# Rows of the matmuls' moving operands 32 bytes further apart

## The chip, the cores and the metric

The kernel runs on one core of a Trainium2 chip. The core has a matrix engine (TensorE, PE in the profile, with its weight loads shown apart as PEld), a vector engine (DVE), a scalar engine (ACT), GpSimd (POOL) and a sync engine (SP) that issues the DMAs here. Each engine runs its own list of instructions, and semaphores hold it where it needs another's result. A matmul on PE takes a weight block of 128 x 128 values that a weight load puts in place, and streams a second operand past it, the moving operand: here 256 columns, mostly. Both lie in the on-chip memory SBUF, which has 128 partitions; "address" below is a byte within a partition, the same in all of them. Results go to the accumulator memory PSUM.

The metric is the time of one execution on the device in microseconds, shorter being better.

## The reference, cut to what matters

A backbone of two layers is run on two groups of tokens that share the parameters: 128 context tokens and 128 latent tokens, which here lie side by side as the 256 columns of every moving operand. Layer 0 mixes tokens with multi-head latent attention and grouped-query attention side by side, layer 1 with differential attention; both are followed by a gated feed-forward part with a short convolution. What the changed rows feed are the large projections:

```python
h = rmsnorm(x, g_norm_mix[l]) * (1 + sc1) + sh1      # 2048 features
m, new = mixer_ab(h, ...)   # proj = h @ w_in ... out = concat(out_a, out_b) @ w_out
x = x + gt1 * m
h = rmsnorm(x, g_norm_ffn[l]) * (1 + sc2) + sh2
u = h @ w_up                                          # 2048 -> 2 * 5632
u = conv3(u) + b_conv; gate, val = split(u)
x = x + gt2 * ((silu(gate) * val) @ w_down)           # 5632 -> 2048
```

All inputs and outputs are float32.

## The kernel before, in words

**Two halves of every operand.** TensorE takes a reduced float32 format (`F32R`), so the kernel splits each operand into a rounded part and the rest: `split` copies the source into the high part on ACT (L194) and subtracts it on DVE for the low part (L195). `gemm` then makes three matmuls for each block k of 128 input features: high weights by high activations (L240), high weights by low activations (L241), low weights by high activations (L242), all added up in one PSUM bank. The next block follows directly. Each matmul has its own weight load, so in time the load for the next matmul runs beside the streaming of this one.

**Where the operands lie.** Weights come by DMA into `raw` (8 KB of a partition), are split into the tiles `wh` and `wl` of eight blocks of 512 bytes each, four buffers of each. Activations lie in three tiles whose rows (one for each k) hold 256 high values, then 256 low ones, 2048 bytes in all:

- `hx`, 16 rows: the normalised and modulated input of the mixers and of both feed-forward parts (`modulate`, L439 on ACT and L441 on DVE or POOL), and, under the same tag, the attention output `o` of layer 0 (`head_ab`);
- `oall`, 16 rows: the attention output of layer 1;
- `g`, 22 tiles of one row: the gated activations of half a feed-forward part, which the down projection reads.

The tiles `ql` and `kv_in` of layer 0's second projections are built in the same way, and the change leaves them alone.

In the compiled program the first row of `hx` lies at byte 43616, the `g` tiles from byte 182752 on in steps of 2048, `oall` at 163392, the `wh` buffers at 118752 and every 4096 after it, `wl` at 135136 and every 4096 after it. A row of 2048 bytes, a low half 1024 bytes behind its high half, a weight block of 512 bytes and a weight buffer of 4096 are all multiples of 512. So the distance of a moving row's start from a weight block's start, taken modulo 512, is one number for a whole tile: 128 for `hx`, 0 for `g`, 96 for `oall`. "Place" below means this number.

**Order.** The program runs layer 0's mixer (stage "ab", to about 500 us), its feed-forward part ("ffn0", to about 1250), layer 1's mixer ("c", to about 1700) and its feed-forward part ("ffn1"). In a feed-forward part, `up` (matmuls on `hx`) and `down` (matmuls on `g`) alternate, each twice. The order of work on every engine is decided when the program is built, by tile dependencies and a planner that places the modulation work (`row_step`, `feature_step`) between the projections; it does not depend on addresses. The gemms' results are taken from PSUM by ACT or DVE, with three buffers.

```python
pe.matmul(ps[:, :n], wh, xh(k), start=(i == 0), stop=False)
pe.matmul(ps[:, :n], wh, xl(k), start=False, stop=False)
pe.matmul(ps[:, :n], wl, xh(k), start=False, stop=(i == last))
```

Of the kernel before, what the change touches and what calls it, by code (L numbers as in the profile page):

```python
# [10 lines left out]
F32 = mybir.dt.float32  # L11
# [8 lines left out]
KD = D // P  # L20
T = 128
NT = 2 * T
NL = 2
GRID_W = 64
EPS = 1e-6
# [49 lines left out]
def step_kernel(ctx: ExitStack, tc: tile.TileContext, A: dict):  # L75
# [22 lines left out]
    def T_(pl, shape, tag, dt=F32, bufs=None):  # L98
        kw = {} if bufs is None else {"bufs": bufs}
        return pl.tile(shape, dt, tag=tag, name=nm(tag), **kw)  # L100
# [92 lines left out]
    def split(out_hi, out_lo, src):  # L193
        act.copy(out_hi, src)  # L194
        dve.tensor_tensor(out=out_lo, in0=src, in1=out_hi.bitcast(F32), op=ALU.subtract)  # L195
# [229 lines left out]
    def modulate(hx, rb, l, which, chunks):  # L425

        for c in chunks:
            h = T_(tmp, [P, NT], "nt", bufs=4)
            dve.tensor_tensor(out=h, in0=x[:, c], in1=rb, op=ALU.mult)
            for g in range(2):  # L430
                s = slice(g * T, (g + 1) * T)
                a_ = scl[:, l, which, c, g:g + 1]
                b_ = mod[:, l, 3 * which, c, g:g + 1]
                if g == 0:
                    dve.tensor_scalar(out=h[:, s], in0=h[:, s], scalar1=a_, scalar2=b_,  # L435
                                      op0=ALU.mult, op1=ALU.add)
                else:
                    act.activation(h[:, s], h[:, s], AF.Identity, scale=a_, bias=b_)
            act.copy(hx[:, c, :NT], h)  # L439
            eng = pool if c % 2 else dve  # L440
            eng.tensor_tensor(out=hx[:, c, NT:], in0=h, in1=hx[:, c, :NT].bitcast(F32),  # L441
                              op=ALU.subtract)

    def modulated(st, l, which, units):
        ensure(l, 3 * which + 1)
        ensure(l, 3 * which)
        hx = T_(keep, [P, KD, 2 * NT], "hx", F32R)
        modulate(hx, norm_scale(st), l, which, range(KD))
        fill(units)
        return hx  # L450
# [48 lines left out]
    def head_ab(pl, pairs, rs, v, hx, c):  # L499

        s = T_(ppool["att"], [P, 512], "att", bufs=3)
        for g, ks in ((0, slice(0, T)), (1, slice(T, 3 * T))):
            for i, (q, k) in enumerate(pairs):
                pe.matmul(s[:, ks], q[:, g * T:(g + 1) * T], k[:, ks],  # L504
                          start=(i == 0), stop=(i == len(pairs) - 1))
        mx = T_(small, [P, 2], "mx")
        sums = T_(small, [P, 2], "sums")
        p = T_(pl, [P, 3 * T], "p", bufs=2)
        softmax_parts(s, mx, sums, rs, None, p)
        rec = T_(small, [P, 2], "rec")  # L510
        dve.reciprocal(out=rec, in_=sums)
        dve.tensor_scalar(out=p[:, :T], in0=p[:, :T], scalar1=rec[:, 0:1], scalar2=None, op0=ALU.mult)
        dve.tensor_scalar(out=p[:, T:], in0=p[:, T:], scalar1=rec[:, 1:2], scalar2=None, op0=ALU.mult)
        yield
        pT = transposed(pl, p)
        yield
        o = T_(ppool["att"], [P, 512], "att", bufs=3)
        pe.matmul(o[:, 0:T], v(0), pT[:, 0:T], start=True, stop=True)
        pe.matmul(o[:, T:NT], v(1), pT[:, T:2 * T], start=True, stop=False)
        pe.matmul(o[:, T:NT], v(2), pT[:, 2 * T:], start=False, stop=True)  # L520
        split(hx[:, c, :NT], hx[:, c, NT:], o[:, :NT])


    def mixer_ab(hx, rb0, st):
        l = 0
        with tc.tile_pool(name="ab", bufs=1) as ab:
            with tc.tile_pool(name="abp", bufs=1) as pj:
# [106 lines left out]
                for q in range(4):  # L634
                    ensure(0, 1, [q])
                    ensure(0, 0, [q])
                    ada["both"] = False
                    pinned[0] = q == 3
                    if q == 3:
                        caches()  # L640
                    modulate(hx, rb0, 0, 0, range(4 * q, 4 * q + 4))
                    for c in range(23):
                        ps = gemm(W.chunk(), lambda k: hx[:, 4 * q + k, :NT], lambda k: hx[:, 4 * q + k, NT:])
                        to = pr[:, c] if c < 15 else qb[:, c - 15]
                        if q == 0:
                            act.copy(to, ps)
                        else:
                            dve.tensor_tensor(out=to, in0=to, in1=ps, op=ALU.add)
                        if q == 3:
                            finish(c)  # L650
                        if q < 3:
                            pump(RATE["in"], until=2 * (q + 2))
                        else:
                            pump(RATE["in3"])

            with tc.tile_pool(name="abh", bufs=1) as hp:
                ada["pew"] = PEW["heads"]

                o = T_(keep, [P, KD, 2 * NT], "hx", F32R)
                load_cw(0)  # L660
                WQ = Weights(A["w_q_up"], 6, 2)
                WK = Weights(A["w_kv_up"], 4, 4)
# [67 lines left out]
        ensure(l, 2)  # L730
        ada["pew"] = PEW["out0"]
        W = Weights(A["w_out_ab"], KD, 1)
        oh, ol = (lambda k: o[:, k, :NT]), (lambda k: o[:, k, NT:])
        for c in range(KD):
            fine[0] = c >= KD - QUIET[1]
            residual(gemm(W.chunk(), oh, ol, first=8), l, 0, c, st)
# [3 lines left out]
    def mixer_c(cp, hx, st):  # L740
# [10 lines left out]
                                 op0=ALU.add, op1=ALU.subtract)  # L751

        W = Weights(A["w_in_c"], KD, 1)
        xh, xl = (lambda k: hx[:, k, :NT]), (lambda k: hx[:, k, NT:])
        outs = []
        o_all = T_(cp, [P, KD, 2 * NT], "oall", F32R)

        def project(h):
            q = T_(cp, [P, 2, NT], "dq", bufs=2)
# [27 lines left out]
        def attend(h, q, k, v):  # L787
# [47 lines left out]
                    pe.transpose(pt[:, i * NT + g * T:i * NT + (g + 1) * T],  # L835
                                 on[:, g, i * P:(i + 1) * P], ident)
            src = pt.rearrange("p (i t) -> p i t", i=2)
            split(o_all[:, 2 * h:2 * h + 2, :NT], o_all[:, 2 * h:2 * h + 2, NT:], src)

        for h in range(8):  # L840
            start(attend(h, *project(h)))
# [1 line left out]

        ensure(l, 2)
        W = Weights(A["w_out_c"], KD, 1)
        oh, ol = (lambda k: o_all[:, k, :NT]), (lambda k: o_all[:, k, NT:])
        for c in range(KD):
            fine[0] = c >= KD - QUIET[2]
            residual(gemm(W.chunk(), oh, ol), l, 0, c, st)
# [5 lines left out]


    def ffn(hx, l, st):
        xh, xl = (lambda k: hx[:, k, :NT]), (lambda k: hx[:, k, NT:])
        W = Weights(A["w_up"][l], KD, 1)
        WD = Weights(A["w_down"][l], KQ, TB)  # L860
        cw = ada["cw"]
        with tc.tile_pool(name=f"ffn{l}", bufs=1) as fp, banks(f"pffn{l}") as pf:
            feat["home"], feat["pool"] = fp, pf

            def conv(ps, m):
                y = T_(fp, [P, NT], "cv", bufs=3)
                act.activation(y, ps, AF.Identity, scale=cw[:, 1, m:m + 1], bias=cw[:, 3, m:m + 1])  # L867
                y3 = y.rearrange("p (g t) -> p g t", g=2)
                p3 = ps.rearrange("p (g t) -> p g t", g=2)
                dve.scalar_tensor_tensor(out=y3[:, :, 1:], in0=p3[:, :, :T - 1],  # L870
                                         scalar=cw[:, 0, m:m + 1], in1=y3[:, :, 1:],
                                         op0=ALU.mult, op1=ALU.add)
                dve.scalar_tensor_tensor(out=y3[:, :, :T - 1], in0=p3[:, :, 1:],  # L873
                                         scalar=cw[:, 2, m:m + 1], in1=y3[:, :, :T - 1],
                                         op0=ALU.mult, op1=ALU.add)
                return y

            def up(q):
                gs = []
                for i in range(q * KQ, (q + 1) * KQ):  # L880
                    rate = 0 if i < LATE else FRATE["up"]
                    fine[0] = False
                    gate = conv(gemm(W.chunk(), xh, xl), i)
                    pump(0, rate)
                    if i == 0:
                        load_row()
                    val = conv(gemm(W.chunk(), xh, xl), NFF + i)
                    pump(0, rate)
                    act.activation(gate, gate, AF.Silu)
                    dve.tensor_tensor(out=val, in0=gate, in1=val, op=ALU.mult)  # L890
                    g = T_(fp, [P, 2 * NT], "g", F32R, bufs=KQ)
                    split(g[:, :NT], g[:, NT:], val)
                    gs.append(g)
                return gs

            def down(gs, q):
                for c in range(KD):
                    quiet = q == NQ - 1 and c >= KD - QUIET[0]
                    fine[0] = quiet
                    ps = gemm(WD.chunk(), lambda k: gs[k][:, :NT], lambda k: gs[k][:, NT:])  # L900
                    residual(ps, l, 1, c, st if q == NQ - 1 else None)
                    pump(0, 0 if quiet else FRATE["down"])

            for q in range(NQ):
                gs = up(q)
                if q == 0:
                    ensure(l, 5)
                down(gs, q)
            while feat["i"] < FLIMIT[stage[0]]:
                feature_step()  # L910


    with banks("pab") as ppool["ada"]:
# [5 lines left out]
        st = stat_init()  # L919
        for c in range(KD):  # L920
            stat_add(st, x[:, c], KD)
        hx = T_(keep, [P, KD, 2 * NT], "hx", F32R)
        rb0 = norm_scale(st)
        st = stat_init()
        mixer_ab(hx, rb0, st)
# [150 lines left out]
```

## Time and profile before

| what | us |
|---|---|
| median of three runs | 2488.23 |
| lowest and highest | 2485.64, 2488.37 |
| the profiled execution, whole | 2491.76 |
| its span, first to last instruction | 2489.7 |
| PE busy in it | 2424.8 (97%) |
| DVE busy | 1767.7 (71%) |
| ACT busy | 1155.9 (46%) |
| POOL busy | 167.2 (7%) |

The profiled execution lies 3.5 us above the median of the runs. Matmuls are pipelined: one is shown as 0.28 us long while the next starts about 0.12 us after it, so the sum of the matmuls' lengths says nothing of the time they take; the distance between starts does. How many matmuls start in a window of known length gives that distance. A count of a window also holds those that were still running at its left edge, 0.28 / 0.12, or 2.4 on average.

### The profile page before, as it was taken

What the parts mean: (1) busy time and instruction counts of PE and PEld (TensorE: products, weight loads), DVE (VectorE), ACT (ScalarE), POOL (GpSimd) and SP (SyncE); (2) the same over time, 40 slices, a digit from 0 to 9 for tenths busy, and PEclk for the clock granted to TensorE, in tenths of its full rate; (3) what the DMA queues carried; (4) which work ended last, traced back from release to release, by engine and by line L of the source; (5) the groups of instructions that cost most, each with busy time, mean ns of one, the idle gap of its engine ahead of it and who ended that gap; (6) DMA issues with size and microseconds to landing.
All of it is one profiled execution on the core that took longest, in us unless ns stands there. A gap on an engine that the chain in (4) does not pass through costs nothing.

```text
span 2489.7 us, 47301 instructions
## 1 busy us (share of the span) xinstructions
PE 2424.8 (97%) x19664; PEld 2284.3 (92%) x19664; DVE 1767.7 (71%) x2699; ACT 1155.9 (46%) x1815; POOL 167.2 (7%) x211
## 2 busy tenths in 40 slices
PE   6999999999999999999999999999999999999997
PEld 4778768799999999999979999897999999999997
DVE  2457534578898999999869897766897655666644
ACT  4335544455453345544455454345555434555442
POOL 2002101100000000001110101021000000000011
PEclk9999999999999999999999999999999999999999
DMA  9886677876667767677776777757665555555553
GB/s 380 310 318 242 233 266 305 307 267 252 253 251 266 300 255 259 252 268 259 279 272 246 271 250 277 265 206 284 245 236 185 185 185 187 187 187 185 182 179 115
DMA packets 92549, 612.92 MB, mean 246 GB/s; under 512 B 9968, under 2 KB 17840, under 8 KB 20400
## 3 DMA queue, kind: packets, MB, share of 16 engines
q1 hardware_dynamic: 92336, 609.91, 66.9%
q8 instruction: 154, 2.52, 0.4%
q14 instruction: 59, 0.48, 0.1%
HBM read 605.12 MB, written 4.75 MB: 245 GB/s over the span
## 4 chain that ended last, share of the span: by engine, by line
PE 94%; DMA 2%; issue 1%; DVE 1%; ACT 1%; POOL 0%; POOLq 0%; SPq 0%; DVEq 0%; ACTq 0%
PE acc L240 29%; PE acc L241 29%; PE acc L242 29%; PE ada L333 4%; DMA araw<-w_ada 1%; PE att L504 1%; DMA ckc<-cache_ckv 1%; PE ada L281 1%; DMA raw<-w_in_ab 0%; PE att L794 0%; PE att L494 0%; DMA raw<-w_ada 0%; DVE x L945 0%; PE ada L268 0%; DVE nt L435 0%
## 5 line engine op out<-in xcount | busy, mean ns | idle before, releaser
L194 ACT CAST wh<-raw 128x1024 fp32r<-128x1024 f32 (+1 forms) x788 | 791.8, 1010 | 1116.3 <-PE acc L241 956.1
L195 DVE TENSOR_TENSOR wl<-raw,wh 128x1024 fp32r<-128x1024 f32 (+1 forms) x788 | 924.9, 1182 | 469.1 <-ACT wh L194 466.4
L240 PE MATMUL acc<-hx,wh 128*128 128x256 f32 x4208 | 1191.5, 285 | 10.2 <-ACT hx L439 9.5
L241 PE MATMUL acc<-hx,wh 128*128 128x256 f32 x4208 | 1190.3, 283 | 0.0
L242 PE MATMUL acc<-hx,wl 128*128 128x256 f32 x4208 | 1189.3, 283 | 0.0
L240 PEld LDWEIGHTS acc<-hx,wh 128*128 128x128 f32 x4208 | 793.7, 189 | 47.5 <-ACT hx L439 19.7
L241 PEld LDWEIGHTS acc<-hx,wh 128*128 128x128 f32 x4208 | 795.0, 189 | 21.0 <-issue 19.4
L242 PEld LDWEIGHTS acc<-hx,wl 128*128 128x128 f32 x4208 | 795.2, 189 | 12.2 <-issue 12.1
L241 PE MATMUL acc<-g,wh 128*128 128x256 f32 x1408 | 398.1, 283 | 0.0
L242 PE MATMUL acc<-g,wl 128*128 128x256 f32 x1408 | 397.9, 283 | 0.0
L240 PE MATMUL acc<-g,wh 128*128 128x256 f32 x1408 | 397.7, 283 | 0.0
L318 DVE CUSTOM_DVE_ANT_0 junk<-araw,condb 128x2048 f32<-128x2048 f32 x120 | 274.8, 2290 | 0.0
L241 PEld LDWEIGHTS acc<-g,wh 128*128 128x128 f32 x1408 | 270.3, 192 | 0.0
L242 PEld LDWEIGHTS acc<-g,wl 128*128 128x128 f32 x1408 | 270.2, 192 | 0.0
L240 PEld LDWEIGHTS acc<-g,wh 128*128 128x128 f32 x1408 | 270.1, 192 | 0.0
L160 POOL TENSOR_TENSOR sqacc<-sqacc,sq 128x256 f32<-128x256 f32 x76 | 88.0, 1158 | 1613.1 <-issue 1282.1
L333 PE MATMUL ada<-araw,condw 128*32 128x512 f32 x864 | 124.4, 651 | 20.4 <-DMA araw<-w_ada 19.6
L362 DVE SCALAR_TENSOR_TENSOR aacc<-araw,condw,aacc 128x512 f32<-128x512 f32 x150 | 107.8, 748 | 0.3
L455 DVE SCALAR_TENSOR_TENSOR x<-acc,mod,x 128x128 f32<-128x128 f32 x192 | 58.3, 345 | 63.2 <-PE acc L242 63.2
L867 ACT ACTIVATE cv<-acc,convw 128x256 f32<-128x256 f32 x176 | 98.6, 560 | 0.0
L873 DVE SCALAR_TENSOR_TENSOR cv<-acc,convw,cv 128x254 f32<-128x254 f32 x176 | 84.3, 479 | 3.7
L870 DVE SCALAR_TENSOR_TENSOR cv<-acc,convw,cv 128x254 f32<-128x254 f32 x176 | 83.7, 476 | 0.0
(195 smaller groups left out, 1625.9 us busy)
## 6 DMA issues: line engine op xcount, KB each, us to landing
araw<-w_ada SPq DMA_DIRECT2D x188, 1024.0 KB, 5.9
raw<-w_up SPq DMA_DIRECT2D x176, 1024.0 KB, 4.8
raw<-w_down SPq DMA_DIRECT2D x88, 1024.0 KB, 4.8
raw<-w_in_c SPq DMA_DIRECT2D x48, 1024.0 KB, 5.1
raw<-w_in_ab SPq DMA_DIRECT2D x20, 1024.0 KB, 7.2
raw<-w_out_ab SPq DMA_DIRECT2D x16, 1024.0 KB, 5.2
raw<-w_out_c SPq DMA_DIRECT2D x16, 1024.0 KB, 4.8
raw<-w_q_up SPq DMA_DIRECT2D x6, 768.0 KB, 4.7
```

The costliest lines, as they stand in the source:

```text
L160: pool.tensor_tensor(out=st["acc"], in0=st["acc"], in1=sq, op=ALU.add)
L194: act.copy(out_hi, src)
L195: dve.tensor_tensor(out=out_lo, in0=src, in1=out_hi.bitcast(F32), op=ALU.subtract)
L240: pe.matmul(ps[:, :n], wh, xh(k), start=(i == 0), stop=False)
L241: pe.matmul(ps[:, :n], wh, xl(k), start=False, stop=False)
L242: pe.matmul(ps[:, :n], wl, xh(k), start=False, stop=(i == last))
L318: tc.keep_in_program_order(dve.tensor_tensor_reduce(out=T_(feat["pool"], [P, D], "junk"), in1=feat["row"][:, c], in0=feat["raw"].rearrange ...
L333: i = pe.matmul(ada["ps"][32 * g:32 * g + 32, :], condw[:, 4 * t + g, :], raw[:, g], start=(t == 0), stop=(t == 3), skip_group_check=True)
L362: i = dve.scalar_tensor_tensor(out=acc[:, c], in0=raw[:, g], scalar=condw[:, k, c:c + 1], in1=acc[:, c], op0=ALU.mult, op1=ALU.add)
L867: act.activation(y, ps, AF.Identity, scale=cw[:, 1, m:m + 1], bias=cw[:, 3, m:m + 1])
L870: dve.scalar_tensor_tensor(out=y3[:, :, 1:], in0=p3[:, :, :T - 1], scalar=cw[:, 0, m:m + 1], in1=y3[:, :, 1:], op0=ALU.mult, op1=ALU.add)
L873: dve.scalar_tensor_tensor(out=y3[:, :, :T - 1], in0=p3[:, :, 1:], scalar=cw[:, 2, m:m + 1], in1=y3[:, :, :T - 1], op0=ALU.mult, op1=ALU.add)
```

## The change

A constant `ROW = 2 * NT + 8` replaces the row length of 512 values in the three tiles, so a row takes 2080 bytes, with 32 bytes unused at its end. The high half stays at the row's start and the low half 1024 bytes behind it; the slices that ran to the row's end now stop at 512.

```diff
+ROW = 2 * NT + 8
...
-            eng.tensor_tensor(out=hx[:, c, NT:], in0=h, in1=hx[:, c, :NT].bitcast(F32),
+            eng.tensor_tensor(out=hx[:, c, NT:2 * NT], in0=h, in1=hx[:, c, :NT].bitcast(F32),
...
-        hx = T_(keep, [P, KD, 2 * NT], "hx", F32R)
+        hx = T_(keep, [P, KD, ROW], "hx", F32R)
...
-                        ps = gemm(W.chunk(), lambda k: hx[:, 4 * q + k, :NT], lambda k: hx[:, 4 * q + k, NT:])
+                        ps = gemm(W.chunk(), lambda k: hx[:, 4 * q + k, :NT], lambda k: hx[:, 4 * q + k, NT:2 * NT])
...
-                o = T_(keep, [P, KD, 2 * NT], "hx", F32R)
+                o = T_(keep, [P, KD, ROW], "hx", F32R)
...
-        o_all = T_(cp, [P, KD, 2 * NT], "oall", F32R)
+        o_all = T_(cp, [P, KD, ROW], "oall", F32R)
...
-                    g = T_(fp, [P, 2 * NT], "g", F32R, bufs=KQ)
-                    split(g[:, :NT], g[:, NT:], val)
+                    g = T_(fp, [P, ROW], "g", F32R, bufs=KQ)
+                    split(g[:, :NT], g[:, NT:2 * NT], val)
```

The list of instructions of each engine, their order and their waits stay the same; only addresses differ. `hx` still begins at byte 43616 and grows by 512 bytes, and every tile behind it, the weights among them, moves up by 512 bytes. So weight blocks keep their addresses modulo 512, and the place of row k of `hx` becomes 128 + 32 k modulo 512: over its 16 rows each multiple of 32 comes once. The 22 rows of `g` and the 16 of `oall` step in the same way.

More of the change, by code (lines that the diff above doesn't have):

```diff
@@ L520, in head_ab @@
         pe.matmul(o[:, T:NT], v(2), pT[:, 2 * T:], start=False, stop=True)
-        split(hx[:, c, :NT], hx[:, c, NT:], o[:, :NT])
+        split(hx[:, c, :NT], hx[:, c, NT:2 * NT], o[:, :NT])
     def mixer_ab(hx, rb0, st):
@@ L732, in mixer_ab @@
         W = Weights(A["w_out_ab"], KD, 1)
-        oh, ol = (lambda k: o[:, k, :NT]), (lambda k: o[:, k, NT:])
+        oh, ol = (lambda k: o[:, k, :NT]), (lambda k: o[:, k, NT:2 * NT])
         for c in range(KD):
@@ L753, in mixer_c @@
         W = Weights(A["w_in_c"], KD, 1)
-        xh, xl = (lambda k: hx[:, k, :NT]), (lambda k: hx[:, k, NT:])
+        xh, xl = (lambda k: hx[:, k, :NT]), (lambda k: hx[:, k, NT:2 * NT])
         outs = []
-        o_all = T_(cp, [P, KD, 2 * NT], "oall", F32R)
+        o_all = T_(cp, [P, KD, ROW], "oall", F32R)
         def project(h):
@@ L837, in attend @@
             src = pt.rearrange("p (i t) -> p i t", i=2)
-            split(o_all[:, 2 * h:2 * h + 2, :NT], o_all[:, 2 * h:2 * h + 2, NT:], src)
+            split(o_all[:, 2 * h:2 * h + 2, :NT], o_all[:, 2 * h:2 * h + 2, NT:2 * NT], src)
         for h in range(8):
@@ L845, in mixer_c @@
         W = Weights(A["w_out_c"], KD, 1)
-        oh, ol = (lambda k: o_all[:, k, :NT]), (lambda k: o_all[:, k, NT:])
+        oh, ol = (lambda k: o_all[:, k, :NT]), (lambda k: o_all[:, k, NT:2 * NT])
         for c in range(KD):
@@ L857, in ffn @@
     def ffn(hx, l, st):
-        xh, xl = (lambda k: hx[:, k, :NT]), (lambda k: hx[:, k, NT:])
+        xh, xl = (lambda k: hx[:, k, :NT]), (lambda k: hx[:, k, NT:2 * NT])
         W = Weights(A["w_up"][l], KD, 1)
@@ L899, in down @@
                     fine[0] = quiet
-                    ps = gemm(WD.chunk(), lambda k: gs[k][:, :NT], lambda k: gs[k][:, NT:])
+                    ps = gemm(WD.chunk(), lambda k: gs[k][:, :NT], lambda k: gs[k][:, NT:2 * NT])
                     residual(ps, l, 1, c, st if q == NQ - 1 else None)
@@ L921, in step_kernel @@
             stat_add(st, x[:, c], KD)
-        hx = T_(keep, [P, KD, 2 * NT], "hx", F32R)
+        hx = T_(keep, [P, KD, ROW], "hx", F32R)
         rb0 = norm_scale(st)
```

## The prediction

> **What bounds the kernel now.** I read the page's busy shares first, then the chain that ended last, then the groups by line.
>
> ```profile
> PE 2424.8 (97%) x19664; PEld 2284.3 (92%) x19664; DVE 1767.7 (71%) x2699; ACT 1155.9 (46%) x1815; POOL 167.2 (7%) x211
> ...
> PE 94%; DMA 2%; issue 1%; DVE 1%; ACT 1%; POOL 0%; POOLq 0%; SPq 0%; DVEq 0%; ACTq 0%
> ...
> L240 PE MATMUL acc<-hx,wh 128*128 128x256 f32 x4208 | 1191.5, 285 | 10.2 <-ACT hx L439 9.5
> L241 PE MATMUL acc<-hx,wh 128*128 128x256 f32 x4208 | 1190.3, 283 | 0.0
> L242 PE MATMUL acc<-hx,wl 128*128 128x256 f32 x4208 | 1189.3, 283 | 0.0
> ...
> L241 PE MATMUL acc<-g,wh 128*128 128x256 f32 x1408 | 398.1, 283 | 0.0
> L242 PE MATMUL acc<-g,wl 128*128 128x256 f32 x1408 | 397.9, 283 | 0.0
> L240 PE MATMUL acc<-g,wh 128*128 128x256 f32 x1408 | 397.7, 283 | 0.0
> ```
>
> PE is busy 97% of the span and carries 94% of the chain. Nearly all of its work is one form, 128 x 256, three matmuls for each weight block: 3 x 4208 = 12,624 read `hx` and 3 x 1408 = 4,224 read `g`. PE waited 10.2 us in all before the first group and not at all before the others, so a nanosecond more or less between two starts goes into the time undiminished. The rows of `oall` come from the groups with shapes kept apart, and with them the writers of the moved rows:
>
> ```profile
> L240 PE MATMUL acc<-oall,wh 128*128 128x256 f32 x256 | 73.8, 290 | 0.7 <-ACT oall L194 0.7
> ...
> L195 DVE TENSOR_TENSOR g<-cv,g 128x256 fp32r<-128x256 f32 x88 | 36.7, 417 | 0.0
> L194 ACT CAST g<-cv 128x256 fp32r<-128x256 f32 x88 | 35.0, 397 | 0.0
> L441 POOL TENSOR_TENSOR hx<-nt,hx 128x256 fp32r<-128x256 f32 x32 | 28.0, 884 | 200.2 <-ACT hx L439 200.2
> L439 ACT CAST hx<-nt 128x256 fp32r<-128x256 f32 x64 | 22.8, 399 | 3.4 <-DVE nt L435 3.1
> ```
>
> That is 3 x 256 = 768 more, 17,616 matmuls on changed rows.
>
> **What a matmul takes today, by place.** Windows in which PE does nothing else, PE's instructions alone: two on `hx` (feed-forward up), one on `g` (down), one on `oall` (layer 1's output projection). The columns are window, its length, PE busy with its count, granted clock (1.00 is full), DMA share, GB/s:
>
> ```profile
> 560.00:660.00 100.00, 100.00 (x845) 1.00 0.67 245
> ...
> 1640.00:1690.00 50.00, 50.00 (x419) 1.00 0.52 189
> ...
> 2150.00:2300.00 150.00, 150.00 (x1266) 1.00 0.52 183
> 2350.00:2450.00 100.00, 100.00 (x836) 1.00 0.52 181
> ```
>
> A count also holds the 2.4 matmuls that ran into the window. So starts lie 150,000 / (1266 - 2.4) = 118.71 ns apart on `hx` (100,000 / 842.6 = 118.68 in the other window, where the DMAs move a third more), 100,000 / (836 - 2.4) = 119.96 on `g`, 50,000 / (419 - 2.4) = 120.02 on `oall`. The form, the lines, the clock and the weight tiles are the same; the tile read differs, and with it the place: 128, 0 and 96. The timeline shows that this is no average over stalls. Starts in us, then the length; five on `hx`, then five on `g`:
>
> ```profile
> 1000.05 0.28 PE L240 MATMUL acc<-hx,wh 128*128 128x256 f32 x1
> 1000.17 0.28 PE L241 MATMUL acc<-hx,wh 128*128 128x256 f32 x1
> 1000.28 0.28 PE L242 MATMUL acc<-hx,wl 128*128 128x256 f32 x1
> 1000.40 0.28 PE L240 MATMUL acc<-hx,wh 128*128 128x256 f32 x1
> 1000.52 0.28 PE L241 MATMUL acc<-hx,wh 128*128 128x256 f32 x1
> ...
> 2000.77 0.28 PE L242 MATMUL acc<-g,wl 128*128 128x256 f32 x1
> 2000.89 0.28 PE L240 MATMUL acc<-g,wh 128*128 128x256 f32 x1
> 2001.01 0.28 PE L241 MATMUL acc<-g,wh 128*128 128x256 f32 x1
> 2001.13 0.28 PE L242 MATMUL acc<-g,wl 128*128 128x256 f32 x1
> 2001.25 0.28 PE L240 MATMUL acc<-g,wh 128*128 128x256 f32 x1
> ```
>
> On `g` every step is 0.12 us. On `hx` a step of 0.11 comes in between, and the position in the triple (L240, L241, L242) does not decide where: something that repeats, and that the place has a part in, sets the pace. The weight loads keep step with it:
>
> ```profile
> 1000.05 0.19 PEld L241 LDWEIGHTS acc<-hx,wh 128*128 128x128 f32 x1
> 1000.17 0.19 PEld L242 LDWEIGHTS acc<-hx,wl 128*128 128x128 f32 x1
> 1000.29 0.19 PEld L240 LDWEIGHTS acc<-hx,wh 128*128 128x128 f32 x1
> ```
>
> The load for the next matmul starts with the streaming of this one (1000.05, 1000.17, 1000.28 against 1000.05, 1000.17, 1000.29), so the two reads whose distance the change alters do run side by side.
>
> **The change, part by part.** *Instructions and order*: none is added, taken away or moved, on any engine or queue; the DMAs do not touch the padded tiles. No wait is added. This costs nothing.
>
> *The writers of the rows* (L194, L195, L439, L441) write the same 256 values, 32 bytes further on for each row. I cost that at nothing: their 88 + 88 + 32 + 64 instructions above come to 122.5 us in all, and PE waits only 9.5 us for them, at the starts of stages. Were each 1% slower, the most on the path would be 0.1 us. If the cover were gone, 1% would be 1.2 us.
>
> *Memory*: `hx` and `oall` grow by 512 bytes a partition, 22 `g` tiles by 704; the number of buffers stays, so no load is issued later than before.
>
> *The gaps between matmuls* are the whole sum. Each tile will run through 16 places, three matmuls at each. Three of the 16 have a price: 118.71, 119.96 and 120.02 ns. Thirteen have none. For these I take the mean of the three, 119.56, since no row says which of the three the unknown ones resemble, and they lie within 1.3 ns of each other though 0, 96 and 128 are far apart. Then
> - `hx`: 12,624 x (119.56 - 118.71) = +10.7 us;
> - `g`: 4,224 x (119.56 - 119.96) = -1.7 us;
> - `oall`: 768 x (119.56 - 120.02) = -0.4 us.
>
> The sum is +8.6 us. The profiled execution of 2491.76 would become 2500.4; it lies 3.5 above the median of the runs, so the median should go from 2488.23 to 2496.8. The loss, if it comes, comes from `hx`: today it sits on the best of the three known places.
>
> Bounds from the same rows: if all places were like 128, `g` and `oall` would gain 4,224 x 1.25 + 768 x 1.31 = 6.3 us, 2481.9. If all were like 0 and 96, `hx` would lose 12,624 x 1.27 = 16.0 us, 2504.2. [...]
>
> [...]
>
> [...]
>
> **The rivals.**
>
> *Faster: the unknown places are better.* `hx` has one step of 0.11 us now and then, `g` none; if the walk gave one more such step in every five, the mean would be 118.71 - 10 / 5 = 116.7. That is 12,624 x 2.0 + 4,224 x 3.3 + 768 x 3.3 = 41.7 us less: 2446.5. [...] Against it: the three seen show no place near 116. It decides once the mean over all places falls below today's mean of 119.07 (12,624 at 118.71, 4,992 at 119.97).
>
> *Clearly slower: the step itself costs.* Each third matmul changes the place, 17,616 / 3 = 5,872 times. If the pattern has to find itself anew and one matmul then takes 0.13 instead of 0.12 us, that is 58.7 us on top of the sum: 2555.5. For it: `hx` keeps a repeating pattern now, and such a change breaks it. Against it: on `g` there is no pattern to lose.
>
> *Nothing happens: the place has no part in it.* The gaps stay, and the time is 2488.2. [...] Against it: the two tiles differ by 1.25 ns and I see nothing else that differs between them.
>
> **How the numbers follow.** The mean of the known places gets 0.56. Its own range is 2482 to 2506; by the prices at its two ends most of it is slower: 0.46 slower, 0.07 within 0.2%, 0.03 faster. The better places get 0.23, all faster. The cost of the step gets 0.13, all slower. No effect gets 0.08, within. Together faster 0.26, same 0.15, slower 0.59. The bound of 0.2%, 5 us here, is about what a measurement of this kernel can tell, whose three runs lie within 2.7 us. A range for 8 in 10 has to cut into both outer cases: half of the faster rival's gain, 2465, and half of the step's cost, 2526.
>
> **What would show it.** In the changed kernel's profile the counts of PE alone, in windows of a feed-forward up, should fall from 1266 in 150 us to some 1257, in a down window rise from 836 in 100 us to about 839; the granted clock and the groups' counts should stay. The timeline should show steps that change from row to row of `hx` and repeat with the 16 rows. The prediction is wrong if the unseen places are not like the three: an up window above 1290 means the first rival, below 1235 the second, 1266 the third. It is also wrong if an interval appears that depends on the row before, for then a mean over places says nothing.

## The result, and the profile after

The changed kernel takes 2474.53 us (median of four runs, 2471.96 to 2475.53), the kernel before 2487.5 beside it: a ratio of 0.9947 with a 95% interval of 0.993 to 0.9965. It is faster by 0.5%. The forecast was 2496.8, slower by 0.35%; the time lies inside the stated range of 2465 to 2526, but on the other side of no change.

The profiled execution took 2474.37 us with a span of 2472.3, 17.4 us less than before. Its page, with the lines one further down than before because of the new constant:

```profile
PE 2408.7 (97%) x19664; PEld 2268.5 (92%) x19664; DVE 1766.5 (71%) x2699; ACT 1156.3 (47%) x1815; POOL 170.4 (7%) x211
...
PE 94%; DMA 2%; issue 1%; DVE 1%; ACT 1%; POOL 0%; POOLq 0%; SPq 0%; DVEq 0%; ACTq 0%
...
L241 PE MATMUL acc<-hx,wh 128*128 128x256 f32 x4208 | 1192.7, 285 | 10.9 <-ACT hx L440 10.1
...
L243 PE MATMUL acc<-g,wl 128*128 128x256 f32 x1408 | 394.4, 281 | 0.0
```

PE lost 16.1 us of busy time, 2424.8 to 2408.7, with the same number of instructions; POOL was busy 3.2 us longer, and DVE, ACT, PE's share of the chain and the wait before the first group are nearly what they were. So the gain lies between the starts of the matmuls. PE's windows (window, length, PE busy and count, granted clock, DMA share, GB/s): three on `hx`, `oall` in the third row, `g` in the last.

```profile
560.00:660.00 100.00, 100.00 (x848) 1.00 0.69 248
900.00:1000.00 100.00, 100.00 (x848) 1.00 0.70 257
1630.00:1670.00 40.00, 40.00 (x340) 1.00 0.54 186
2150.00:2300.00 150.00, 150.00 (x1270) 1.00 0.54 189
2350.00:2450.00 100.00, 100.00 (x853) 1.00 0.47 163
```

With 2.4 taken off each count, starts are 150,000 / 1267.6 = 118.33 ns apart on `hx` (118.71 before), 100,000 / 850.6 = 117.56 on `g` (119.96 before) and 40,000 / 337.6 = 118.48 on `oall` (120.02 before). By the numbers of matmuls that is 12,624 x 0.38 = 4.8 us, 4,224 x 2.40 = 10.1 and 768 x 1.54 = 1.2: together 16.1, of the 17.4 that the two profiled executions differ by. All three tiles gained, `g` the most for each matmul and `hx` the least.

The timeline of the changed kernel in the middle of a row sequence of `hx`: start in us, then the length.

```profile
1002.84 0.28 PE L242 MATMUL acc<-hx,wh 128*128 128x256 f32 x1
1002.96 0.28 PE L243 MATMUL acc<-hx,wl 128*128 128x256 f32 x1
1003.07 0.28 PE L241 MATMUL acc<-hx,wh 128*128 128x256 f32 x1
1003.19 0.28 PE L242 MATMUL acc<-hx,wh 128*128 128x256 f32 x1
...
1004.26 0.28 PE L242 MATMUL acc<-hx,wh 128*128 128x256 f32 x1
1004.38 0.28 PE L243 MATMUL acc<-hx,wl 128*128 128x256 f32 x1
1004.49 0.28 PE L241 MATMUL acc<-hx,wh 128*128 128x256 f32 x1
```

Steps of 0.11 and 0.12 us follow each other in a new order. Worked out from all starts, the order repeats after 24 matmuls, that is after eight rows or 256 bytes of walk, not after sixteen rows: the mean step on a row of `hx` and on the row 256 bytes further on agree within 0.15 ns for all eight pairs. So places are taken modulo 256 from here on. The cheapest row is the one at 192, 116.1 ns in the mean, the dearest the one at 32, 119.5.

### The profile page after: what moved, and what is told of

It is laid out like the page before. It is cut to its first block, busy times and chain, and to the rows that moved or that the text cites. A ratio compares the mean times of both kernels' runs of the same rounds, so it can differ in the third digit from the quotient of the medians.

```text
span 2472.3 us, 47301 instructions
## 1 busy us (share of the span) xinstructions
PE 2408.7 (97%) x19664; PEld 2268.5 (92%) x19664; DVE 1766.5 (71%) x2699; ACT 1156.3 (47%) x1815; POOL 170.4 (7%) x211
## 4 chain that ended last, share of the span: by engine, by line
PE 94%; DMA 2%; issue 1%; DVE 1%; ACT 1%; POOL 0%; POOLq 0%; SPq 0%; DVEq 0%; ACTq 0%
PE acc L241 29%; PE acc L242 29%; PE acc L243 29%; PE ada L334 4%; DMA araw<-w_ada 1%; PE att L505 1%; DMA ckc<-cache_ckv 1%; PE ada L282 1%; DMA raw<-w_in_ab 0%; PE att L795 0%; DMA raw<-w_ada 0%; PE att L495 0%; DVE x L946 0%; PE ada L269 0%; DVE nt L436 0%
## 5 line engine op out<-in xcount | busy, mean ns | idle before, releaser
L241 PE MATMUL acc<-hx,wh 128*128 128x256 f32 x4208 | 1192.7, 285 | 10.9 <-ACT hx L440 10.1
L241 PE MATMUL acc<-g,wh 128*128 128x256 f32 x1408 | 393.9, 280 | 0.0
L242 PE MATMUL acc<-g,wh 128*128 128x256 f32 x1408 | 393.6, 280 | 0.0
L242 PEld LDWEIGHTS acc<-g,wh 128*128 128x128 f32 x1408 | 265.3, 188 | 0.0
L243 PEld LDWEIGHTS acc<-g,wl 128*128 128x128 f32 x1408 | 265.1, 188 | 0.0
L241 PEld LDWEIGHTS acc<-g,wh 128*128 128x128 f32 x1408 | 264.7, 188 | 0.0
```

## The experiments

All kernels compute the whole result, and the instructions of each engine and their order are those of the changed kernel in every one; only addresses differ. They start from its text. Where the rows are 2048 bytes apart again, the first line of the diff is

```diff
-ROW = 2 * NT + 8
+ROW = 2 * NT
```

and three paddings set the places. Values behind the rows of `hx` move everything that lies behind it, the weights among it, and so lower the place of `hx`; values behind `condb` raise the place of `g`; values ahead of `oall`'s rows raise that of `oall`:

```diff
-T_(keep, [P, KD, ROW], "hx", F32R)
+T_(keep, [P, KD * ROW + 48], "hx", F32R)[:, :KD * ROW].rearrange("p (k n) -> p k n", k=KD)
...
-T_(feat["home"], [P, 2, D], "condb")
+T_(feat["home"], [P, 2 * D + 8], "condb")[:, :2 * D].rearrange("p (r n) -> p r n", r=2)
...
-T_(cp, [P, KD, ROW], "oall", F32R)
+T_(cp, [P, KD * ROW + 120], "oall", F32R)[:, 120:].rearrange("p (k n) -> p k n", k=KD)
```

Two theories stood against each other. By the first, each place has a price, and the prediction merely guessed the unseen ones wrongly. By the second, the gain belongs to the walk itself: it keeps the stream from settling into the repeating steps of a fixed place.

### Standing still at the unseen places

The padding shown above (48, 8 and 120 values) puts `hx` at 192, `g` at 32, `oall` at 64.

> Rows 2048 bytes apart again, so every row of a tile has one place, as before the change; but the places are moved by padding ahead of the tiles: hx from 128 to 192 (taken modulo 256), g from 0 to 32, oall from 96 to 64. Place theory (each place has its price, wherever it is met; prices are the means by row of the changed kernel): hx 116.1 ns between starts, g 119.5, oall 119.1, time about 2453 us. Walk theory (the price belongs to walking; a tile that stays at one place falls back to the 118.7 to 120.0 seen before): hx 118.7 or more, time about 2488 us. Prediction's theory (the unseen places are like the three seen): the same as the walk theory here, 2480 to 2505.

It took 2419.12 us (2416.36 to 2421.64), a ratio of 0.9723 with an interval of 0.9707 to 0.974. That is 34 us below even the place theory's 2453. Two windows of `hx`, one of `oall` and one of `g`:

```profile
560.00:660.00 100.00, 100.00 (x885) 1.00 0.74 270
900.00:1000.00 100.00, 100.00 (x885) 1.00 0.73 270
...
1594.20:1654.20 60.00, 60.00 (x512) 1.00 0.54 191
...
1990.00:2040.00 50.00, 50.00 (x431) 1.00 0.54 190
```

`hx` stands at 100,000 / 882.6 = 113.3 ns, lower than the row at 192 in the walk (116.1) and lower than any window shown above; `oall` at 60,000 / 509.6 = 117.7, `g` at 50,000 / 428.6 = 116.7. The walk theory falls: a fixed place can be much better than the walk. The prediction's reason falls too, that the unseen places are like the seen ones. The place theory has the right sign and, for `hx`, the right best place, but the price that a place has in the walk is not the one that it has at rest.

The second kernel has 40, 40 and 8 values of padding: `hx` at 224, `g` at 160, `oall` at 128.

> Rows 2048 bytes apart, places hx 224, g 160, oall 128 (modulo 256). Place theory: hx 117.2 ns, g 117.6, oall 119.0; time about 2459 us. Walk theory: all between 118.7 and 120.0, time about 2488 us. A check that the place counts and not the tile: oall at 128 should show the 118.7 that hx had there before, and not the 120.0 it had at 96.

It took 2478.43 us (ratio 0.9959, interval 0.9945 to 0.9974). Windows on `hx`, on `oall` and on `g`:

```profile
900.00:1000.00 100.00, 100.00 (x847) 1.00 0.69 252
1630.00:1660.00 30.00, 30.00 (x255) 1.00 0.55 194
1990.00:2040.00 50.00, 50.00 (x423) 1.00 0.55 190
```

That is 118.4 ns at 224, 118.8 at 128, 118.9 at 160. `oall` at 128 has the price that `hx` had there (118.7), not its own old one of 120.0. The prices taken from the walk, 117.2 at 224 and 117.6 at 160, were too low.

The third has 16, 56 and 24 values: `hx` at 64, `g` at 224, `oall` at 192.

> Rows 2048 bytes apart, places hx 64, g 224, oall 192 (modulo 256). Place theory: hx 119.1 ns, g 117.2, oall 116.1; time about 2479 us. Walk theory: all between 118.7 and 120.0, time about 2488 us. g at 224 and hx at 224 (another run of this call), oall at 192 and hx at 192, should agree with each other if the place alone counts.

It took 2461.74 us (2453.19 to 2464.43; ratio 0.9887, interval 0.9865 to 0.9909). Two windows on `hx`, one on `oall`, one on `g`:

```profile
560.00:660.00 100.00, 100.00 (x884) 1.00 0.73 265
900.00:1000.00 100.00, 100.00 (x851) 1.00 0.72 263
1630.00:1660.00 30.00, 30.00 (x268) 1.00 0.56 198
1990.00:2040.00 50.00, 50.00 (x425) 1.00 0.53 184
```

`oall` at 192 steps by 30,000 / 265.6 = 113.0 (113.3 by the starts of its longest stretch) and `g` at 224 by 118.3, as `hx` did at these places. But `hx` at 64 shows two prices in one execution: 113.4 in the first feed-forward up, 117.8 in the next and in all later ones; in the short stretches of the mixers both come up, by the starts. Neither theory had that.

The fourth has 24, 16 and 16 values and puts other tiles at places known from one tile: `hx` at 32, `g` at 64, `oall` at 160.

> Rows 2048 bytes apart, places hx 32, g 64, oall 160: three places that another tile held in an earlier run (g 116.7 at 32; hx at 64 with 113.3 in the first feed-forward up and 117.8 from the second on; g 118.7 at 160). If the place sets the price whatever the tile: hx 116.7 in all feed-forward windows, oall 118.7, and g one of the two values of 64. If the tile, its number of rows or the stage sets it: hx away from 116.7 by over 0.5. Time by the first: 2488.3 - 12,624 x 2.0 - 4,224 x (2.2 to 6.7) - 768 x 1.3 ns = 2434 to 2453 us.

Two windows on `hx`, two on `g` in its second down, one on `oall`, one on `g` in its third down, then a late one on `hx`:

```profile
560.00:660.00 100.00, 100.00 (x860) 1.00 0.69 252
900.00:1000.00 100.00, 100.00 (x836) 1.00 0.70 253
...
1122.00:1202.00 80.00, 80.00 (x708) 1.00 0.75 277
1213.00:1242.00 29.00, 29.00 (x249) 1.00 0.79 284
...
1630.00:1660.00 30.00, 30.00 (x258) 1.00 0.53 181
1990.00:2040.00 50.00, 50.00 (x427) 1.00 0.53 184
2120.00:2220.00 100.00, 100.00 (x860) 1.00 0.54 187
```

At 32 `hx` steps by 116.6, then by 120.0 for a whole up, then by 116.6 again. At 64 `g` steps by 80,000 / 705.6 = 113.4 in most of its second down, after an interruption of under 1 us (at 1211) by 29,000 / 246.6 = 117.6 to the end of it, and by 117.8 in the other three. `oall` at 160 steps by 30,000 / 255.6 = 117.4, where `g` in still_b had 118.9. So the expectation that the place alone sets the price, with 116.7 in every up and 118.7 on `oall`, is not met. The two executions of this one kernel took 2463.26 and 2438.29 us, which leaves its ratio between 0.9713 and 0.9965. The price of a place is thus not always one number: at 64 there are two, and both `hx` and `g` show both; at 32 `hx` shows two in the feed-forward parts, and `g` in still_a one of them. In these executions one of them held for a whole uninterrupted stretch, and a change came only between stretches. What picks one of them was not tried.

### The walk in the other direction

`hx` walks by +32 a row, but `g`, whose tiles are handed out from high addresses to low ones, by -32 (and +160 once), so it does not step in the same way, as the section on the change has it. That could be why `g` came out lower than `hx`. This kernel turns both: rows of `hx` from the last to the first, `g` as one tile in rising order, with the 2080-byte rows of the changed kernel.

```diff
-            act.copy(hx[:, c, :NT], h)
+            act.copy(hx[:, KD - 1 - c, :NT], h)
...
-        xh, xl = (lambda k: hx[:, k, :NT]), (lambda k: hx[:, k, NT:2 * NT])
+        xh, xl = (lambda k: hx[:, KD - 1 - k, :NT]), (lambda k: hx[:, KD - 1 - k, NT:2 * NT])
...
-                    g = T_(fp, [P, ROW], "g", F32R, bufs=KQ)
+                    g = gt[:, i - q * KQ]
...
+            gt = T_(fp, [P, KQ, ROW], "g", F32R)
```

> The changed kernel with the direction of the walk turned round: the rows of hx are laid down in falling order, so its place falls by 32 from row to row instead of rising, and the rows of g are laid down in rising order, so its place rises instead of falling; oall is left rising. Order of instructions unchanged. Direction theory (a falling walk is cheaper, as g at 117.6 ns against hx at 118.3 and oall at 118.3 suggests): hx falls to 117.6, g rises to 118.3, time about 2474.5 - 12,624 x 0.7 ns + 4,224 x 0.7 ns = 2469 us. Place theory (only the set of places counts): hx 118.3 and g 117.6 stay, 2474.5 us.

It took 2471.85 us (2470.11 to 2474.68; ratio 0.9935, interval 0.992 to 0.9949). A window on `hx` and one on `g`:

```profile
900.00:1000.00 100.00, 100.00 (x853) 1.00 0.68 253
...
1990.00:2040.00 50.00, 50.00 (x424) 1.00 0.53 181
```

`hx` fell to 117.6 ns and `g` rose to 118.6, as the direction theory said; `oall`, left rising, stayed at 118.4 by its starts. The two changes go against each other: they come to 12,624 x 0.7 - 4,224 x 1.0 = 4.6 us less, the medians lie 2.7 us apart, and the executions of the two kernels overlap, so the time alone would not tell. Why a falling walk is cheaper is not shown. In the rising walk of the changed kernel the first matmul on each row of `hx` steps by 119.3 ns in the mean and the other two by 117.7 and 117.8; in the falling walk of `g` all three lie between 117.5 and 117.8. In the turned kernel `g`, rising now, has 119.2 on the first and 118.2 and 117.9 on the others. So the extra sits where the place rises.

### What the place is measured against

In the first of these two kernels everything moves by 32 bytes together, with rows of 2048 bytes.

```diff
-    cst = T_(keep, [P, NCONST], "cst")
+    cst = T_(keep, [P, NCONST + 8], "cst")[:, :NCONST]
```

> The kernel before with one tile ahead of all others 32 bytes longer: operands, weights and everything else move up by 32 bytes together, all places stay (hx 128, g 0, oall 96). Place theory: hx 118.7, g 120.0, oall 120.0 as before, time that of the kernel before within 0.2%. Address theory (it is the address of a row by itself that has the price, since 32 bytes change whether it starts at a multiple of 64): other numbers, and the time moves by 0.5% or more.

It took 2487.18 us (ratio 0.9991, interval 0.9981 to 1.0001). Windows on `hx` and on `g`:

```profile
900.00:1000.00 100.00, 100.00 (x845) 1.00 0.71 262
...
1990.00:2040.00 50.00, 50.00 (x419) 1.00 0.53 182
```

These are the counts of the kernel before, 118.7 and 120.0 ns. It is a distance that has the price, not an address.

In the second a tile of 64 bytes between `wh` and `wl` moves the low weights, and all that lies behind them. The other paddings are 48, 48 and 24 values, so that without the tile all would stand at 192.

```diff
+                        if not self.at > 1 and "gap" not in ada:
+                            ada["gap"] = T_(wpool, [P, 16], "gap", bufs=1)
                         wl_ = T_(wpool, [P, 1024], "wl", F32R, bufs=4)
```

> Rows 2048 bytes apart; the low weights lie 64 bytes further on than the high ones, so each tile has two places, one against the high and one against the low weights: hx 192 and 128, g and oall 0 and 192. Load theory (a matmul's stream is held up by the load of the next weights, which runs beside it): the stream at L242, beside which the low weights are loaded, has the odd place, so on g the step from L242 to L243 is the short one and the mean is near (120 + 113.5 + 120) / 3 = 117.8, on hx it is the long one, mean near (114 + 118.7 + 114) / 3 = 115.5. Own-weights theory (the stream minds the place of the weights that it uses): the odd step is the one from L243 to L241. Place does not matter against the low weights: hx 114.0, g 120.0.

It took 2475.52 us (ratio 0.9944, interval 0.9926 to 0.9962). Windows on `hx` (192 against the high weights, 128 against the low) and on `g` (0 and 192):

```profile
900.00:1000.00 100.00, 100.00 (x848) 1.00 0.71 260
...
1990.00:2040.00 50.00, 50.00 (x427) 1.00 0.52 184
```

`hx` steps by 118.3, not by 113.3 as at 192 against both (still_a): moving only the low weights away (`hx` and the high weights stay) cost 5 ns a matmul in the mean. `g` steps by 117.8, the mean that both theories gave. So where the low weights lie counts, and not the high ones alone. By the starts, the means of the steps after the three matmuls of a block, in order, are 119.0, 119.5 and 116.2 on `hx` and 117.5, 117.5 and 118.3 on `g`. The own-weights theory wanted the third step to be the long one on `hx` and the short one on `g`; it is the other way round on both, so it falls. The load theory's second step is the longest on `hx`, but on `g` no shorter than the first, and its sizes are met on neither: it is not borne out. On `hx` the mean of the places (115.5) fails by 2.7 ns, as if going back and forth between two places cost by itself. The tile also changes the distance between the low and the high weights, which no other kernel does. Whether the 5 ns come from the distance of the rows to the low weights or from that one is not separated.

### Finer than 32 bytes, and the best place for all

Here `g` stands at 192 and the rows of `hx` and `oall` 16 bytes to either side of it. The diff is that of the first kernel with 48, 48 and 20 values and the rows of `hx` 4 values into their tile.

> Rows 2048 bytes apart, g at place 192, hx at 208 and oall at 176, half a step of 32 bytes to either side of 192. If the price changes smoothly with the place: hx halfway between 114.0 and 118.35, 116.2; oall halfway between 118.7 and 113.6, 116.1; time about 2432 us. If reads come in aligned pieces of 32 bytes and only the piece counts: hx 114.0 and oall 118.7, or hx 118.35 and oall 113.6. If the optimum lies between the tried places: one of the two below 113.3.

It took 2462.41 us (ratio 0.9891, interval 0.9873 to 0.9909). Windows on `hx` (208), `oall` (176) and `g` (192):

```profile
900.00:1000.00 100.00, 100.00 (x841) 1.00 0.68 248
1630.00:1660.00 30.00, 30.00 (x254) 1.00 0.55 186
1990.00:2040.00 50.00, 50.00 (x443) 1.00 0.54 190
```

119.2 at 208 and 119.2 at 176, against 113.5 for `g` at 192: worse than the neighbours on both sides at 32 bytes, so neither a smooth curve nor a 32-byte grain. Whether that is the place, or a row that begins off a multiple of 32, was not separated.

Last, every tile that a split matmul reads is put at 192: 48, 48 and 24 values, and 48 ahead of `kv_in`, which also moves `ql`.

> Rows 2048 bytes apart, and every tile that a split matmul reads (hx, g, oall, ql, kv_in) at place 192. Place theory with the prices of standing still (hx and oall at 192 showed 114.0 and 113.6): hx 114.0, g about 113.6; against the run with hx at 192 and g at 32 (116.7) that is 4,224 x 3.1 + 768 x 4.2 + some 400 x 6 ns, 18 to 19 us less: about 2401 us. If the good price needs a rhythm of three matmuls and 16 rows that g with its 22 tiles does not offer: g stays at 116 or more, 2410 us or above.

It took 2396.09 us (2393.78 to 2398.73), a ratio of 0.9625 with an interval of 0.9612 to 0.9638: a version that beats both kernels. Its page and its windows, three on `hx` with one on `oall` (third row), the two on `g` at 1920 and 2290:

```profile
PE 2327.3 (97%) x19664; PEld 2188.2 (91%) x19664; DVE 1763.0 (74%) x2699; ACT 1161.4 (49%) x1815; POOL 168.4 (7%) x211
...
PE 92%; DMA 3%; DVE 2%; issue 1%; ACT 1%; POOL 0%; POOLq 0%; SPq 0%; DVEq 0%; ACTq 0%
```

```profile
560.00:660.00 100.00, 100.00 (x885) 1.00 0.72 263
900.00:1000.00 100.00, 100.00 (x885) 1.00 0.74 272
1590.00:1630.00 40.00, 40.00 (x355) 1.00 0.58 206
1920.00:1970.00 50.00, 50.00 (x443) 1.00 0.56 193
2120.00:2220.00 100.00, 100.00 (x884) 1.00 0.56 191
2290.00:2360.00 70.00, 70.00 (x620) 1.00 0.57 196
```

In these windows `hx` and `oall` step by 113.3 to 113.4 and `g` by 113.3 to 113.5, whatever its number of rows. PE is still 92% of the chain, with DVE and the DMAs a point more each, so nearly all of it reached the time. But 192 has a second pace too. Two stretches on `hx` of layer 1's mixer in this execution:

```profile
1278.50:1292.50 14.00, 14.00 (x121) 1.00 0.67 244
1299.00:1313.00 14.00, 14.00 (x126) 1.00 0.67 236
```

The first steps by 14,000 / 118.6 = 118.0 ns (117.8 by its starts), the second by 14,000 / 123.6 = 113.3. Here, and in the mixers of still_a, 117.8 came up only in short stretches; `hx` ran at 113.3 in all feed-forward parts. `ql`, at place 0 in the kernel before, went from 119.5 to 115.6 in the mean of its starts.

## Why the prediction was wrong, point by point

**What bounds the kernel**: right. With the same instructions PE got 16.1 us shorter and the profiled execution 17.4. In the best version its 97.5 us less of busy time stand beside 92 us less in the median.

**Instructions, order, writers, memory at no cost**: right. The tile view of the changed kernel has the writers of `g` at the medians they had in that of the kernel before, 397 and 418 ns:

```profile
L195 ACT CAST g<-cv x88: 388/397/403, 515.3 to 2337.0; 128x256 fp32r<-128x256 f32 x88
L196 DVE TENSOR_TENSOR g<-cv,g x88: 413/418/421, 516.0 to 2338.3; 128x256 fp32r<-128x256 f32 x88
```

**"The gaps between matmuls are the whole sum"**: right, and so was the reading that place is behind the 118.71 and 119.96. Kernels that differ in nothing but places range from 2396 to 2488 us.

**The step that failed**: "Thirteen have none. For these I take the mean of the three, 119.56". In its place the runs show 118.33 on `hx`, 117.56 on `g`, 118.48 on `oall`; the terms +10.7, -1.7 and -0.4 became -4.8, -10.1 and -1.2. Two things were wrong in the step. The places come again after 256 bytes, so there are eight and not sixteen, and the three known are, at rest, among the dearest: of the eight that 256 bytes allow, 0 and 96 stand at 120.0 and 128 at 118.7, while the unseen five stand at 113.3 (192, apart from its short stretches), 113.4 or 117.8 (64), 116.6 or 120.0 (32), 117.4 or 118.9 (160; 117.4 is `oall` in still_e, 30,000 / 255.6) and 118.4 (224). With the lower value where there are two the mean of the eight is 117.2, with the higher one 118.4; the walks lie at 117.6 to 118.6. And a mean over places at rest is not the price of a walk: the same eight places cost 118.3 rising and 117.6 falling. Three values close together were taken as a sign that all places are alike. They were three draws, two of them at the top of the list. That the unseen places are cheaper is shown by the kernels that stand still; how much of the walk's gain comes from that, and how much from walking, is not separated.

**"If all were like 0 and 96" and "all like 128" as bounds**: wrong for the same reason. Both ends came from the known places, and the time fell below the lower one, 2481.9. It lies inside the wider range only because that range was cut into the faster rival, not by the sum. (Half of that rival's gain is 2467, not 2465; the difference changes nothing here.)

**The rivals.** The faster one, that the unseen places are better, had the right sign, and the kernels that stand still bear out its reason; its point of decision, today's mean of 119.07, was right too: the new mean is 118.15 (12,624 at 118.33, 4,992 at 117.70). Its price of 41.7 us was 2.6 times too large, for it set the mean at 116.7. The slower one, that a step costs, is there in small: the first matmul after a rising step takes 1.5 ns more than the other two, 0.15 of the 10 ns assumed, and after a falling step nothing. That nothing happens was excluded by the window on `g`, 836 matmuls before and 853 after. The 2396 and 2488 us differ only in the distance between what is streamed and what is loaded; what couples the two, no run here shows.

**What would show it.** The windows foretold were 1257 matmuls in 150 us and 839 in 100; they came out as 1270 and 853. The warning beside them, that a mean over places says nothing if the step depends on the row before, applied: the same place, 192, costs 116.1 in the walk and 113.3 at rest, and the price of the set depends on the direction.

## What to carry to other kernels

Where matmuls follow each other without a wait, compare the distance of their starts between tiles: here two tiles with the same form and clock but different steps, 118.71 ns on `hx` and 119.96 on `g`, were the sign that an address relation had a price, and the program paid it on 17,616 matmuls. Then measure the relation itself, by shifting a tile with padding in steps of 32 bytes, instead of spreading the accesses over all of it; spreading bought 0.5% here, and the best fixed place 3.75%. Here three known values within 1.3 ns of each other said little about the ones not seen, which go down to 113.3, and the bounds taken from them were not bounds.

## What the runs showed of the hardware that was not expected

- The distance between a matmul's moving row and the weight blocks, modulo 256 bytes, moved the step of a 128 x 128 x 256 matmul between 113.3 ns (`hx` at 192 in all_192) and 120.0 (`g` at 0 in the kernel before), both at a granted clock of 1.00; moving all operands together by 32 bytes changed nothing (118.7 and 120.0 in shifted).
- At some distances the stream had at least two steady paces (113.3 and 117.8 at 64, 116.7 and 120.0 at 32, and in short stretches 117.8 beside 113.3 at 192), kept one for windows of 100 us, and came back in the other after an interruption of under 1 us (`g` in still_e, 113.4 and then 117.6). One kernel with tiles at 32 and 64 took 2438.29 and 2463.26 us in two executions; only the second was traced, so that the paces made the difference is likely, not shown.
- Rows 16 bytes off the best place lost all of it (119.2 against 113.3), though 32 bytes off it cost 118.4 on one side and 117.4 or 118.9 on the other.
- The best place did nothing for another shape: the 384-column matmuls on `kv_in` step by 174.2 ns at place 0 and by 174.3 at 192, in the mean of the starts that follow each other directly.
